# The start of a hybrid decoder step: the first product's weights in two halves, its first 24 matmuls ahead of x's third piece, and half of x's sums rebuilt on GpSimd

## The chip, the cores and the metric

The kernel runs on one core of a Trainium2 chip. The metric is the device time of one execution in microseconds (us), median of several. Engines are named as the profile names them: PE is TensorE (PEld its weight loads), DVE is VectorE, ACT is ScalarE, POOL is GpSimd, SP the engine whose queue issues most transfers.

## What is computed

One layer of a decoder over 512 prompt tokens and 8 x 4 sample tokens (544 columns in all), model width 2048. The input x is multiplied by `w_in` (2048 x 18952), whose columns are the queries, keys, values and gates of two parallel branches: an mLSTM with 4 heads and a windowed attention with 32 query and 4 key/value heads. The branches are gated, projected (`w_proj_m`, `w_proj_a`), merged, multiplied by `w_out`, added to x and normalised. The part that matters here is the first step of it:

```python
u = jnp.einsum('btd,dc->btc', x, w_in)      # all projections of x
q_m, k_m, v_m, o_m, z_m, q_a, k_a, v_a, z_a, g_m, g_a, i_pre, f_pre = split(u)
```

## The kernel before

**Arithmetic.** Every fp32 operand is held as a high part (a cast to the reduced format fp32r on ACT, `hi`) and a low part (the operand minus the high part, on DVE, `lo`). A product of weights w and activations x is three matmuls per 128-deep slice k: wh·xh, wh·xl, wl·xh. `split` makes wh and wl of half a weight tile (8 slices, 128 x 1024): one ACT cast (L200) and one DVE subtraction (L201). `hilo` does the same for activations (L245, L246). `products` issues the three matmuls for 8 slices and for the two halves of the 544 columns (272 each), all on L210: 48 matmuls for half a weight tile.

**Start.** x comes in five transfers over its 2048 columns: 256, 256, 512, 512, 512 wide (L307), on SP's queue, in slices k of 128 columns: pieces one and two hold k = 0, 1 and 2, 3, piece three k = 4 to 7. Behind piece two stands the first half of the first product's weights (`raw0[0]`, 512 KB), behind piece four the second half. The sample rows come on ACT's queue (L300). After 20 warm-up transposes (L295) the loop over `g` from 0 to 7 takes two slices each: four PE transposes per slice into a PSUM bank (L328; four such banks, pool `sm`), then `hilo` from PSUM into the activation tiles `a11` and `a21` (k < 8: first and second half of the columns) or `xk2` (k of 8 and more). The sample rows' transposes (L331) stand at k = 2 and fill a bank of their own, which is read out a quarter at a time, at every odd `g`.

**Sums of x.** Later products run in a scheme with seven half products (`paired`, L718) whose activations are sums and differences of x's quarters. Three fp32 tiles gather them: `n2r` = first half of the columns for k < 8 (rebuilt from high and low part on POOL, L351), `s1r` = second half for k < 8 (copied by ACT from PSUM: L337, L348), `n3r` = n2r + s1r (POOL, L359). When k of 8 and more arrive, DVE replaces s1r by x minus s1r (L342, L355). Afterwards `x_sums` (L573) takes s1r from n2r on POOL (L576) and makes high and low parts s1, n3 and n2, the low parts on DVE (L246, L586).

**First products.** `gemm` (L224) is called twice (L613) for the attention values (`VA_`, 128 columns each): first product, into two `bank` tiles, with the weights raw0[0] and raw0[1]; second product with raw0[2] and a later load, with the gate pre-activations (`gates_half`, L395, matmuls on L409) between. The split of the first weights is placed behind the cast of k = 3 (`state["k3"]`). Then come the paired products, L685 (wh) and L687 (wl), which fill most of the kernel; weight sums for them are made by DVE (L665) or by an adding transfer that POOL issues (L663).

**Gates.** `gates` (L412) is a generator that makes small rows of 4 partitions step by step beside the paired products; four DVE copies (L508 to L511) gather rows into `T1`, which PE transposes later (L530).

**Order.** Each engine runs its own queue in order. A planner lays the queues out when the program is built, by program order, priorities and modelled times; `tc.high_priority` lifts a block, and `tc.issue_after(ins)` puts a block's instructions behind `ins` where they are on the same engine. Waits between engines follow from the data.

Of the kernel before, what the change touches and what calls it, by code (L numbers as in the profile page):

```python
# [21 lines left out]
SEQ = 512  # L22
# [52 lines left out]
def _build(tc, nc, i, o, es):  # L75
# [35 lines left out]
    def r32(ap):  # L111
        return ap.bitcast(F32)
# [81 lines left out]
    def split(raw, p=None, tags=("wh", "wl"), parts=1):  # L194
# [3 lines left out]
        n = 8 // parts  # L198
        for k in range(0, 8, n):
            state["cast"] = A.copy(wh[:, k:k + n], raw[:, k:k + n])  # L200
            state["split"] = V.tensor_tensor(out=wl[:, k:k + n], in0=raw[:, k:k + n], in1=r32(wh[:, k:k + n]),  # L201
                                             op=ALU.subtract)
        return wh, wl

    def products(ps, half, wh, wl, xh, xl, cols, every=8):
        for kk in range(8):
            k = half * 8 + kk
            for n, (a, b) in enumerate(((wh, xh), (wh, xl), (wl, xh))):
                for f, c, w in cols:
                    PE.matmul(ps[f][:, :w], a[:, kk], b(k, c, w),  # L210
                              start=(k == 0 and n == 0), stop=(k == 15 and n == 2))
            if (k + 1) % every == 0:
                tick()

# [5 lines left out]
    def mm():  # L220

        return [bank(), bank()]

    def gemm(wv, c0, xh, xl, cols=EVEN, raws=(None, None), every=8, prio=0, before=None, parts=(1, 1),  # L224
             ps=None, behind=None):
        ps = ps or mm()
        for half in range(2):
            if before:
                before(half)
            raw = raws[half] or load_half(wv, c0, half)  # L230
            if prio:
                with tc.high_priority(offset=prio):
                    wh, wl = split(raw, parts=parts[half])
            else:
                with tc.issue_after(behind.ins) if behind and half == 0 else ExitStack():
                    wh, wl = split(raw, parts=parts[half])
            products(ps, half, wh, wl, xh, xl, cols, every)
        return ps

# [4 lines left out]
    def hilo(src, hi, lo, eng=None):  # L244
        state["x_cast"] = A.copy(hi, src)  # L245
        (eng or V).tensor_tensor(out=lo, in0=src, in1=r32(hi), op=ALU.subtract)  # L246
# [41 lines left out]
    def two_k(ch):  # L288
        return slice(ch * 2, ch * 2 + 2)
# [23 lines left out]
    state["load"] = xdma  # L313
# [6 lines left out]
    for t_ in gate_w:  # L320
        G.memset(r32(t_[:]), 0.0)
    pxs = bank()
    for g in range(8):
        for q in range(2):
            k = g * 2 + q
            pt = sm()
            for t in range(4):
                PE.transpose(pt[:, t * 128:t * 128 + 128], xt[k][:, t], ident)  # L328
            if k == 2:
                for c in range(4):  # L330
                    PE.transpose(pxs[:, c * 128:c * 128 + 128], xs[:, c], ident)  # L331
            if k < 8:
                hilo(pt[:, 0:HT], a11[0][:, k], a11[1][:, k])
                hilo(pt[:, HT:SEQ], a21[0][:, k, 0:SEQ - HT], a21[1][:, k, 0:SEQ - HT])
                if k == 3:
                    state["k3"] = state["x_cast"]
                A.copy(s1r[:, k, 0:SEQ - HT], pt[:, HT:SEQ])  # L337
            else:
                hilo(pt[:], xk2[0][k // 4 - 2][:, k % 4, 0:SEQ], xk2[1][k // 4 - 2][:, k % 4, 0:SEQ])
                x_cast = state["x_cast"]  # L340
                c = (slice(None), k - 8, slice(0, SEQ - HT))
                state["x_end"] = V.tensor_tensor(out=s1r[c], in0=pt[:, HT:SEQ], in1=s1r[c], op=ALU.subtract)  # L342
        if g % 2:
            k4 = slice((g // 2) * 4, (g // 2) * 4 + 4)
            src = pxs[:].rearrange("p (c q t) -> p q c t", c=4, q=4)[:, g // 2]
            if g < 4:
                hilo(src, *(a21[p][:, k4, SEQ - HT:HT] for p in range(2)))
                A.copy(s1r[:, k4, SEQ - HT:HT], src)  # L348
                for ch in (g - 1, g):
                    ks_ = two_k(ch)  # L350
                    G.tensor_tensor(out=n2r[:, ks_], in0=r32(a11[0][:, ks_]), in1=r32(a11[1][:, ks_]), op=ALU.add)  # L351
            else:
                hilo(src, *(xk2[p][g // 2 - 2][:, :, SEQ:T] for p in range(2)))
                c = (slice(None), slice(k4.start - 8, k4.stop - 8), slice(SEQ - HT, HT))
                V.tensor_tensor(out=s1r[c], in0=src, in1=s1r[c], op=ALU.subtract)  # L355
        if g == 3:
            for ch in range(4):
                ks_ = two_k(ch)
                G.tensor_tensor(out=n3r[:, ks_], in0=n2r[:, ks_], in1=s1r[:, ks_], op=ALU.add)  # L359
    esXr.close()  # L360
    t544 = pool(esG, "t544", 13)

# [49 lines left out]
    def gates(ps):  # L412
# [95 lines left out]
        V.tensor_copy(T1[0:4, :], ap)  # L508
        V.tensor_copy(T1[32:36, 0:384], A1)
        V.tensor_copy(T1[64:68, 0:256], A2)  # L510
        V.tensor_copy(T1[96:100, 0:128], A3)  # L511
        yield
        A.copy(nM[0:4], M)
        for q in (32, 64):
# [96 lines left out]
            gates_half(gates_ps, half)  # L611

    for kk in range(2):  # L613
        ps = gemm(win, VA_ + kk * 128, xh, xl, raws=((raw0[0], raw0[1]), (raw0[2], None))[kk], every=4, prio=500 * kk,
                  before=gates_between if kk else None, ps=[sm(), sm()] if kk else None, behind=state["k3"])
# [1318 lines left out]
```

## Time and profile before

| what | us |
|---|---|
| median of 3 runs | 2463.73 (2461.29 to 2463.8) |
| the profiled execution | 2463.52 |
| its span in the profile | 2461.7 |

A row of a timeline gives start and duration in us, engine, line of the kernel, operation, output<-input by the program's names, shape and count; where the engine was idle before, the idle time and what ended it stand in brackets. A row of the waits gives who waited for whom, with total, number and longest. A row of a stretch gives its length and, for each engine, busy time and number of instructions, then the granted PE clock (1.00 is full speed), the share of DMA and GB/s. PE instructions overlap in their durations, so the spacing of their starts is their price; the chain of waits shows it as time per group.

### The profile page before, as it was taken

What the parts mean: (1) busy time and instruction counts of PE and PEld (TensorE: products, weight loads), DVE (VectorE), ACT (ScalarE), POOL (GpSimd) and SP (SyncE); (2) the same over time, 40 slices, a digit from 0 to 9 for tenths busy, and PEclk for the clock granted to TensorE, in tenths of its full rate; (3) what the DMA queues carried; (4) which work ended last, traced back from release to release, by engine and by line L of the source; (5) the groups of instructions that cost most, each with busy time, mean ns of one, the idle gap of its engine ahead of it and who ended that gap; (6) DMA issues with size and microseconds to landing.
All of it is one profiled execution on the core that took longest, in us unless ns stands there. A gap on an engine that the chain in (4) does not pass through costs nothing.

```text
span 2461.7 us, 48799 instructions
## 1 busy us (share of the span) xinstructions
PE 2434.9 (99%) x19446; PEld 2381.0 (97%) x19446; DVE 1877.5 (76%) x2813; ACT 1214.4 (49%) x1992; POOL 511.0 (21%) x478
## 2 busy tenths in 40 slices
PE   8999999999999999999999999999999999999997
PEld 8999999999999999999999999999999999999997
DVE  7768888888888887887877888777865654777657
ACT  5456676676676565433433434444633333334431
POOL 3114334333333330221111221211000000110111
PEclk9999999999999999999999999999999999999998
DMA  6876676766666654577687586677755546888876
GB/s 177 198 175 158 159 166 143 164 158 154 160 150 165 152 150 115 152 226 240 180 253 241 164 244 214 182 229 219 248 171 173 185 149 210 223 221 252 220 222 189
DMA packets 555660, 464.72 MB, mean 189 GB/s; under 512 B 43688, under 2 KB 452440, under 8 KB 555176
## 3 DMA queue, kind: packets, MB, share of 16 engines
q1 hardware_dynamic: 538536, 402.09, 55.4%
q0 software_dynamic: 15696, 57.15, 12.1%
q8 instruction: 153, 2.51, 0.4%
q10 hardware_dynamic: 1200, 2.36, 0.3%
q14 instruction: 75, 0.61, 0.1%
HBM read 319.06 MB, written 96.31 MB: 169 GB/s over the span
## 4 chain that ended last, share of the span: by engine, by line
PE 95%; DMA 3%; DVE 1%; issue 1%; ACT 0%; SPq 0%; DVEq 0%; POOL 0%; POOLq 0%
PE bank L685 47%; PE bank L687 23%; PE bank L210 11%; PE sm L1438 2%; PE sm L210 1%; PE bank L1250 1%; PE sm L1470 1%; PE sm L795 1%; PE sm L1483 1%; PE sm L841 1%; DMA tx<-d_y 1%; DMA ty<-d_y 1%; PE sm L1800 1%; PE sm L1255 1%; PE sm L821 1%
## 5 line engine op out<-in xcount | busy, mean ns | idle before, releaser
L200 ACT CAST wh<-raw 128x1024 fp32r<-128x1024 f32 x632 | 662.7, 1049 | 844.5 <-PE bank L685 698.8
L201 DVE TENSOR_TENSOR wl<-raw,wh 128x1024 fp32r<-128x1024 f32 x632 | 790.9, 1252 | 201.9 <-ACT wh L200 184.9
L685 PE MATMUL bank<-xk,wh 128*128 128x272 f32 x2336 | 322.0, 289 | 0.0
L665 DVE TENSOR_TENSOR raw<-raw,raw 128x1024 f32<-128x1024 f32 x238 | 300.9, 1265 | 5.2 <-DMA raw<-in_w_in 1.5
L685 PEld LDWEIGHTS bank<-xk,wh 128*128 128x128 f32 x2336 | 302.8, 188 | 2.0 <-issue 1.5
L704 POOL TENSOR_TENSOR ev<-p,ev 128x272 f32<-128x272 f32 x82 | 118.5, 1446 | 440.2 <-ACT ev L703 397.9
L685 PE MATMUL bank<-n2h,wh 128*128 128x272 f32 x656 | 170.6, 292 | 0.0
L687 PE MATMUL bank<-xk,wl 128*128 128x272 f32 x1168 | 170.1, 288 | 0.0
L685 PE MATMUL bank<-s1h,wh 128*128 128x272 f32 x656 | 169.7, 291 | 0.0
L685 PE MATMUL bank<-n3h,wh 128*128 128x272 f32 x656 | 169.3, 290 | 0.2 <-ACT wh L200 0.2
L685 PE MATMUL bank<-n2l,wh 128*128 128x272 f32 x656 | 168.6, 289 | 0.0
L685 PE MATMUL bank<-n3l,wh 128*128 128x272 f32 x656 | 167.7, 288 | 0.0
L685 PE MATMUL bank<-s4h,wh 128*128 128x272 f32 x656 | 167.6, 289 | 0.0
L685 PE MATMUL bank<-s1l,wh 128*128 128x272 f32 x656 | 167.3, 287 | 0.0
L685 PE MATMUL bank<-s4l,wh 128*128 128x272 f32 x656 | 167.0, 287 | 0.0
L687 PEld LDWEIGHTS bank<-xk,wl 128*128 128x128 f32 x1168 | 155.7, 188 | 0.1
L685 PE MATMUL bank<-a11h,wh 128*128 128x272 f32 x584 | 150.3, 289 | 0.0
L685 PE MATMUL bank<-a11l,wh 128*128 128x272 f32 x584 | 149.5, 288 | 0.0
L210 PE MATMUL bank<-bl,wh 128*128 128x272 f32 x704 | 147.7, 288 | 0.0
L210 PE MATMUL bank<-bh,wl 128*128 128x272 f32 x704 | 147.5, 290 | 0.0
L210 PE MATMUL bank<-bh,wh 128*128 128x272 f32 x704 | 147.3, 288 | 0.0
L663 POOL DMA_DIRECT2D raw<-raw x90 | 78.1, 868 | 291.4 <-DVE ev L712 200.9
(492 smaller groups left out, 5667.0 us busy)
## 6 DMA issues: line engine op xcount, KB each, us to landing
raw<-in_w_in SPq DMA_DIRECT2D x296, 512.0 KB
raw<-raw POOLq DMA_DIRECT2D x90, 512.0 KB, 5.0
C<-in_state_mlstm_C SPq DMA_DIRECT2D x32, 1024.0 KB
out<-C SPq DMA_DIRECT2D x64, 512.0 KB
raw<-in_w_proj_a SPq DMA_DIRECT2D x32, 512.0 KB
raw<-in_w_proj_m SPq DMA_DIRECT2D x32, 512.0 KB
raw<-in_w_out SPq DMA_DIRECT2D x32, 512.0 KB
d_v<-ev SPq DMA_DIRECT2D x16, 272.0 KB
```

Of the source, the lines that this page charges most:

```text
L200: state["cast"] = A.copy(wh[:, k:k + n], raw[:, k:k + n])
L201: state["split"] = V.tensor_tensor(out=wl[:, k:k + n], in0=raw[:, k:k + n], in1=r32(wh[:, k:k + n]), op=ALU.subtract)
L210: PE.matmul(ps[f][:, :w], a[:, kk], b(k, c, w), start=(k == 0 and n == 0), stop=(k == 15 and n == 2))
L663: G.dma_start(out=w[out][:], in_=w[b][:], accum_op=ALU.add)
L665: V.tensor_tensor(out=w[out][:], in0=w[a][:], in1=w[b][:], op=ALU.add)
L685: PE.matmul(ps, wh[:, k], x(p, k), start=(first and k == 0 and p == 0), stop=False, skip_group_check=True)
L687: state["end"] = PE.matmul(ps, wl[:, k], x(0, k), start=False, stop=(k == 7), skip_group_check=True)
L704: G.tensor_tensor(out=c22, in0=p1, in1=c11, op=ALU.subtract)
L795: PE.matmul(pp[:, c0 + w0:c0 + 256], qs[a][:, j * 128:j * 128 + 128], kx[:, k0:k0 + 256 - w0], start=(n == 0), stop=(n == 1))
L821: PE.transpose(pt[:, b * 128:b * 128 + 128], s_[:, b, 128:256], ident)
L841: PE.matmul(po[:, b * 128:b * 128 + n], VA[:, b], p_[:, 2 * b:2 * b + n // 128], start=(b == 0 and m == 0), stop=(b == 3 and m == 1), skip ...
L1438: PE.matmul(pp[:, 0:258], a[:, b * 128:b * 128 + 128], b_[:, b, f], start=(b == 0 and n == 0), stop=(b == 3 and n == 2))
```

## The change

Five edits go together.

- The first weights' half is loaded in two quarters (`load_part` with slices 0 to 3, then 4 to 7): the first behind x's first piece, the second behind x's second piece. `split_part` casts and subtracts one quarter.
- The loop over `g` becomes a function `x_group`, called with the first product's matmuls between: group 0, split of the first quarter, 12 matmuls (k = 0, 1), group 1, 12 matmuls (k = 2, 3), split of the second quarter, groups 2 and 3, 24 matmuls (k = 4 to 7), groups 4 to 7. Group 1's transposes are placed behind the samples' transposes, its casts of the first column half behind the first quarter's cast, and group 2's first transposes behind the 24 matmuls.
- The samples' transposes move from k = 2 to k = 0, and the first read-out of their bank from g = 1 to g = 0.
- ACT no longer copies s1r from PSUM; POOL rebuilds it from a21's high and low part, chunk by chunk between n2r and n3r (four more POOL instructions of 128 x 544).
- The four copies into `T1` move from DVE to POOL.

```diff
         xdma = nc.sync.dma_start(t_, xp_src[:, :, c0:c0 + n])
         xt += [t_[:, :, c:c + 128] for c in range(0, n, 128)]
-        if c0 == 256:
-            raw0.append(load_half(win, VA_, 0))
+        if c0 == 0:
+            raw0.append(wr.tile([128, 8, 128], F32, tag="raw", name=nm("raw")))
+            load_part(raw0[0], win, VA_, 0, slice(0, 4))
+        elif c0 == 256:
+            load_part(raw0[0], win, VA_, 0, slice(4, 8))
         elif c0 == 1024:
             raw0.append(load_half(win, VA_, 1))
...
-    for g in range(8):
+    def x_group(g, behind=None, cast=None):
         for q in range(2):
             k = g * 2 + q
             pt = sm()
             for t in range(4):
-                PE.transpose(pt[:, t * 128:t * 128 + 128], xt[k][:, t], ident)
-            if k == 2:
+                with tc.issue_after(behind.ins) if behind and q == 0 else ExitStack():
+                    PE.transpose(pt[:, t * 128:t * 128 + 128], xt[k][:, t], ident)
+            if k == 0:
                 for c in range(4):
-                    PE.transpose(pxs[:, c * 128:c * 128 + 128], xs[:, c], ident)
+                    state["samples_in"] = PE.transpose(pxs[:, c * 128:c * 128 + 128], xs[:, c], ident)
             if k < 8:
-                hilo(pt[:, 0:HT], a11[0][:, k], a11[1][:, k])
+                with tc.issue_after(cast.ins) if cast else ExitStack():
+                    hilo(pt[:, 0:HT], a11[0][:, k], a11[1][:, k])
                 hilo(pt[:, HT:SEQ], a21[0][:, k, 0:SEQ - HT], a21[1][:, k, 0:SEQ - HT])
-                if k == 3:
-                    state["k3"] = state["x_cast"]
-                A.copy(s1r[:, k, 0:SEQ - HT], pt[:, HT:SEQ])
...
-        if g % 2:
+        if g in (0, 3, 5, 7):
...
-                A.copy(s1r[:, k4, SEQ - HT:HT], src)
-                for ch in (g - 1, g):
-                    ks_ = two_k(ch)
-                    G.tensor_tensor(out=n2r[:, ks_], in0=r32(a11[0][:, ks_]), in1=r32(a11[1][:, ks_]), op=ALU.add)
...
-        if g == 3:
-            for ch in range(4):
+        if g in (1, 3):
+            for ch in (g - 1, g):
                 ks_ = two_k(ch)
+                for r_, (h_, l_) in ((n2r, a11), (s1r, a21)):
+                    G.tensor_tensor(out=r_[:, ks_], in0=r32(h_[:, ks_]), in1=r32(l_[:, ks_]), op=ALU.add)
                 G.tensor_tensor(out=n3r[:, ks_], in0=n2r[:, ks_], in1=s1r[:, ks_], op=ALU.add)
+    ps0 = mm()
+
+    def first_products(k0, k1):
+        products(ps0, 0, *w0, xh, xl, EVEN, ks=slice(k0, k1))
+
+    w0 = [wp.tile([128, 8, 128], F32R, tag=t_, name=nm("wh")) for t_ in ("wh", "wl")]
+    x_group(0)
+    with tc.issue_after(state["x_cast"].ins):
+        split_part(raw0[0], *w0, slice(0, 4))
+    first_products(0, 2)
+    x_group(1, behind=state["samples_in"], cast=state["cast"])
+    first_products(2, 4)
+    with tc.issue_after(state["x_cast"].ins):
+        split_part(raw0[0], *w0, slice(4, 8))
+    for g in range(2, 4):
+        x_group(g, behind=state["product"] if g == 2 else None)
+    first_products(4, 8)
+    for g in range(4, 8):
+        x_group(g)
...
-        V.tensor_copy(T1[0:4, :], ap)
-        V.tensor_copy(T1[32:36, 0:384], A1)
-        V.tensor_copy(T1[64:68, 0:256], A2)
-        V.tensor_copy(T1[96:100, 0:128], A3)
+        G.tensor_copy(T1[0:4, :], ap)
+        G.tensor_copy(T1[32:36, 0:384], A1)
+        G.tensor_copy(T1[64:68, 0:256], A2)
+        G.tensor_copy(T1[96:100, 0:128], A3)
```

`gemm` loses its `parts` and `behind` arguments and gets the halves to run: the first product's call runs its second half only, into `ps0`.

More of the change, by code (lines that the diff above doesn't have):

```diff
@@ L192, in load_half, with split_part, split @@
         return raw
-    def split(raw, p=None, tags=("wh", "wl"), parts=1):
+    def split_part(raw, wh, wl, ks):
+        state["cast"] = A.copy(wh[:, ks], raw[:, ks])
+        state["split"] = V.tensor_tensor(out=wl[:, ks], in0=raw[:, ks], in1=r32(wh[:, ks]), op=ALU.subtract)
+    def split(raw, p=None, tags=("wh", "wl")):
         p = p or wp
@@ L197, in split, with products @@
         wl = p.tile([128, 8, 128], F32R, tag=tags[1], name=nm("wl"))
[L198 to L202, printed above, removed]
+        split_part(raw, wh, wl, slice(0, 8))
         return wh, wl
-    def products(ps, half, wh, wl, xh, xl, cols, every=8):
-        for kk in range(8):
+    def products(ps, half, wh, wl, xh, xl, cols, every=8, ks=slice(0, 8)):
+        for kk in range(ks.start, ks.stop):
             k = half * 8 + kk
@@ L222, in mm, with gemm @@
         return [bank(), bank()]
-    def gemm(wv, c0, xh, xl, cols=EVEN, raws=(None, None), every=8, prio=0, before=None, parts=(1, 1),
-             ps=None, behind=None):
+    def gemm(wv, c0, xh, xl, cols=EVEN, raws=(None, None), every=8, prio=0, before=None, ps=None, halves_=(0, 1)):
         ps = ps or mm()
-        for half in range(2):
+        for half in halves_:
             if before:
@@ L230, in gemm @@
             raw = raws[half] or load_half(wv, c0, half)
[L231 to L236, printed above, removed]
+            with tc.high_priority(offset=prio) if prio else ExitStack():
+                wh, wl = split(raw)
             products(ps, half, wh, wl, xh, xl, cols, every)
```

11 lines of the change are left out of this document (6 added, 5 removed).

## The prediction

> **What bounds the kernel now.** I read the page first: busy time of each engine over the span.
>
> ```profile
> span 2461.7 us, 48799 instructions
> PE 2434.9 (99%) x19446; PEld 2381.0 (97%) x19446; DVE 1877.5 (76%) x2813; ACT 1214.4 (49%) x1992; POOL 511.0 (21%) x478
> ```
>
> TensorE is the bound, and only 26.8 us of the span are its own idle time. A change at the start is therefore worth the TensorE time that it saves there, provided nothing later eats it. The view of waits, for TensorE alone, says where the idle time has a cause (total, times, longest):
>
> ```profile
> PE sm L295 <- DMA cc<-in_consts: 3.3, 1, 3.3
> PE sm L328 <- DMA xr<-in_x_prompt: 3.1, 1, 3.1
> ...
> PE bank L210 <- DVE xk L246: 0.5, 1, 0.5
> ```
>
> The first is the launch, which nothing here touches. The second is the place of the change: the transposes of x's third piece wait for their transfer, and the first product's matmuls stand behind them. Stretches of that stage, with busy time per engine, granted clock, DMA share and GB/s:
>
> ```profile
> 10.45:13.45 3.00, 0.00 (x0) 0.01 (x1) 2.38 (x7) 2.98 (x11) 2.19 (x3) 1.00 1.04 386
> 13.45:14.35 0.90, 0.88 (x8) 0.90 (x9) 0.71 (x2) 0.57 (x3) 0.90 (x1) 1.00 1.05 373
> 14.35:18.15 3.80, 3.80 (x22) 3.80 (x21) 2.49 (x7) 2.83 (x11) 3.76 (x4) 0.56 1.12 343
> ...
> 24.60:30.30 5.70, 5.22 (x44) 5.00 (x42) 5.70 (x11) 5.00 (x11) 2.73 (x2) 1.00 0.51 83
> 30.30:53.70 23.40, 23.38 (x188) 23.37 (x188) 23.40 (x39) 12.33 (x27) 3.39 (x3) 1.00 0.43 111
> ```
>
> Three things stand here. TensorE does nothing for 3.0 us. Right after, its clock is granted at 0.56 for 3.8 us, so 3.8 x 0.44 = 1.7 us more are lost although it counts as busy. And from 24.6 to 53.7 us VectorE is busy without a gap (5.70 of 5.70, 23.40 of 23.40). With the 0.5 us wait for VectorE, the prize is at most 3.0 + 1.7 + 0.5 = 5.2 us, 0.21% of the time.
>
> **The change part by part.** Unit prices first, from the chain of waits (start, us, what):
>
> ```profile
> 23.23 0.45 PE sm L328 x4
> ...
> 46.71 4.03 PE bank L409 x32
> ...
> 53.91 2.00 PE bank L685 x16
> ...
> 56.90 2.00 PE bank L685 x16
> ```
>
> So a transpose costs 0.11 us and a 272-column matmul 0.126 us at full clock; 24 matmuls are 3.0 us.
>
> *Weights in two halves ahead of x's second piece.* TensorE's weight loads show when the first two pieces are there:
>
> ```profile
> 7.42 1.19 PEld L328 LDWEIGHTS sm<-cc,xr 128*128 128x128 f32 x8
> 8.89 0.86 PEld L328 LDWEIGHTS sm<-cc,xr 128*128 128x128 f32 x8 [0.28 <-DMA xr<-in_x_prompt]
> ```
>
> The second piece lands at 8.89 us. A quarter of a megabyte more ahead of it, at the 343 to 386 GB/s of the stretches above, is 0.7 us: 9.6. The extra issue on SP's queue (one of its kind:
>
> ```profile
> 2.20 0.51 SPq L187 DMA_DIRECT2D raw<-in_w_in  x1
> ```
>
> 0.51 us) I put at nothing: the DMA engines are saturated (share above 1), so issues run ahead of them; without that cover it would be half a microsecond on the third piece as well. The bytes ahead of the third piece are unchanged, so it still lands near 13.4. Until 9.6 TensorE does the first piece and the four sample transposes that have moved forward (7.42 + 1.19 + 4 x 0.11 = 9.05), waits 0.55, and does the second piece by 10.5, against 10.42 before: nothing lost.
>
> *The split of the first half, and 24 matmuls ahead of the third piece.* ScalarE, VectorE and GpSimd rows (start, us, instruction):
>
> ```profile
> 8.45 0.82 ACT L245 CAST a11h<-sm 128x272 fp32r<-128x272 f32 x2 [3.22 <-PE sm L328]
> ...
> 11.66 1.05 ACT L200 CAST wh<-raw 128x1024 fp32r<-128x1024 f32 x1
> ```
>
> ```profile
> 12.73 1.23 DVE L201 TENSOR_TENSOR wl<-raw,wh 128x1024 fp32r<-128x1024 f32 x1 [0.61 <-ACT wh L200]
> ...
> 22.77 0.69 DVE L246 TENSOR_TENSOR xk<-sm,xk 128x512 fp32r<-128x512 f32 x1 [1.86 <-ACT xk L245]
> ...
> 25.25 0.68 DVE L246 TENSOR_TENSOR xk<-sm,xk 128x512 fp32r<-128x512 f32 x1
> ...
> 26.16 0.68 DVE L246 TENSOR_TENSOR xk<-sm,xk 128x512 fp32r<-128x512 f32 x1
> ...
> 27.47 2.20 DVE L201 TENSOR_TENSOR wl<-raw,wh 128x1024 fp32r<-128x1024 f32 x1
> ...
> 32.93 0.39 DVE L342 TENSOR_TENSOR r<-sm,r 128x240 f32<-128x240 f32 x1
> ...
> 33.34 2.51 DVE L246 TENSOR_TENSOR s1l<-r,s1h 128x544 fp32r<-128x544 f32 x2
> ```
>
> ```profile
> 9.82 2.64 POOL L351 TENSOR_TENSOR n2r<-a11h,a11l 128x544 f32<-128x544 f32 x2 [6.68 <-DVE a11l L246]
> 13.27 3.20 POOL L359 TENSOR_TENSOR r<-n2r,r 128x544 f32<-128x544 f32 x2 [0.81 <-ACT r L348]
> ...
> 19.65 3.40 POOL L359 TENSOR_TENSOR r<-n2r,r 128x544 f32<-128x544 f32 x2 [0.47 <-ACT r L337]
> 25.41 1.37 POOL L576 TENSOR_TENSOR n2r<-n2r,r 128x544 f32<-128x544 f32 x1 [2.35 <-DVE r L342]
> 27.23 1.35 POOL L576 TENSOR_TENSOR n2r<-n2r,r 128x544 f32<-128x544 f32 x1 [0.45 <-DVE r L342]
> ...
> 33.46 1.81 POOL L576 TENSOR_TENSOR n2r<-n2r,r 128x544 f32<-128x544 f32 x1 [0.44 <-DVE wg L404]
> ```
>
> ScalarE casts the first group from 8.45 and, behind its last piece, half of wh (half of 1.05: 0.55 us), done at about 10.45: in time for the first product at 10.5. The subtraction for wl, 0.65 us by half of 1.23, is another matter. The rows at 27.23 and 27.47 show it: a VectorE instruction with both inputs in SBUF takes 2.20 us instead of 1.23 when a GpSimd add has begun just before it; begun first (12.73), it takes its 1.23 and the add behind it is longer (13.27: 1.60 each against 1.32). I read that as the two shutting each other out, at about 1.0 us a collision. The Trainium skill, "GPSIMD Engine Reference", section "Key points", says the same in kind: GpSimd shares its SBUF interfaces with VectorE, and contends with VectorE instructions that have two SBUF inputs. It gives no price; by it every such pair collides, which is the third rival below. The row at 27.47 bears it out once.
>
> GpSimd's first add again starts near 9.9 us and holds until 11.3. So I take one collision for this first subtraction: wl at 11.95 (bounds: 11.1 with no collision, 13.3 if a second add also gets in ahead). TensorE starts at 10.5, stops after four products, resumes at 11.95 and needs 20 x 0.126 = 2.5 us: 14.45. The third piece, landed at 13.4, is then taken up 1.0 us later than before, but with 24 products done: 3.0 - 1.0 = **2.0 us** gained. No gap exceeds 1 us, so I take the clock as full through 14 to 18 us: **1.7 us** (bounds: nothing, if the clock falls all the same, and 1.7).
>
> *Half of x's sums on GpSimd.* Ten ScalarE copies go (L337, L348); ScalarE isn't the bound here, so they are worth only time for the casts, counted above. Four adds of 1.35 us join eight: 8 x 1.35 + 4 x 1.65 = 17.4 us from 9.9, plus some 2.3 us in which VectorE's splits of weights get in: the last n3r at about 29.6, against 19.65 + 3.40 = 23.05 before. Queued behind this on VectorE are the subtractions into s1r (L342) of the last two chunks of k, and behind them the last low parts of x that TensorE needs. Before, VectorE's stage of k = 8 to 15 ran from 22.77 to 33.3. Now I start it at 20.4 (low parts of k = 4 to 7 until 18.3, the weights' second half until 20.4) and give it 8 x 0.91 (the spacing of 25.25 and 26.16) + 0.4 for samples + 2.2 for a collided split + 0.6 waiting for GpSimd = 10.5: 30.9, so 2.4 us earlier. TensorE comes 3.7 us earlier, so it may wait a little for k = 14 and 15; the next product's matmuls fill most of that. I take 0.3 us off (bounds: 0 and 2).
>
> *What is late next.* At the paired products the split for the second step stands thus:
>
> ```profile
> 53.19 1.05 ACT L200 CAST wh<-raw 128x1024 fp32r<-128x1024 f32 x1 [2.65 <-PE sm L210]
> ```
>
> It ends at 54.24 and TensorE uses it at 56.90 (chain above): 2.66 us of slack. VectorE 2.4 us earlier plus this slack covers a TensorE up to 5.0 us earlier. Beyond, TensorE runs dense, and what it waits for (stores and reloads of its own results) moves with it.
>
> *Four copies into T1 from VectorE to GpSimd.* First and last of four on VectorE, then GpSimd around them:
>
> ```profile
> 84.92 0.42 DVE L508 COPY t<-t 4x544 f32<-4x544 f32 x1
> ...
> 87.10 0.22 DVE L511 COPY t<-t 4x128 f32<-4x128 f32 x1
> ```
>
> ```profile
> 85.93 0.86 POOL L663 DMA_DIRECT2D raw<-raw  x1
> 96.39 0.84 POOL L663 DMA_DIRECT2D raw<-raw  x1 [9.59 <-DMA raw<-in_w_in]
> ```
>
> GpSimd has no such copy in the trace; for 1312 columns together I bound it by nothing and by its 1.35 us per 544 columns, 3.3 us, and take 2. They lie in a gap of 9.59 us; TensorE has no wait there before and none after: nothing. If they are put ahead of the adding transfer at 85.93, that transfer is up to 3.3 us late, and a step's weights with it, of which a slack like the 2.66 us above leaves under 1 us on TensorE.
>
> **Sum:** 2.0 + 1.7 - 0.3 = 3.4 us. The profiled execution took 2463.52 us (span 2461.7, 1.8 around it), so 2460.1. The median of the runs shown is 2463.73, so the two agree within 0.2 us.
>
> **Rivals.**
> 1. *Full recovery.* GpSimd's first add doesn't meet the first subtraction, the 24 products run dense from 10.5 to 13.5, and the 0.5 us at 30 goes too: 3.0 + 1.7 + 0.5 - 0.1 = 5.1 us, **2458.4**. For it: ScalarE has the cast ready in time. Against: VectorE has no idle time to spare from 24.6 on.
> 2. *The products stand ahead but find no weights.* The subtraction is shut out twice (13.3), so TensorE reaches the third piece at 15.8, 2.35 us late: 3.0 - 2.35 + 1.7 - 0.3 = 2.0 us, **2461.5**. The change then does not do what it says. For it: four more adds keep GpSimd busy without a break from 9.9 to 29.6. Against: at 33.34, VectorE's second subtraction followed directly at the add's end (33.46 + 1.81 = 35.27; 33.34 + 2.51 = 35.85).
> 3. *Slower: GpSimd shuts out VectorE through its full stretch.* Besides four splits of weights, eight subtractions for s1l and n3l have both inputs in SBUF. If all twelve collide at 1.0 us, that is eight more than the four in my sum: VectorE is 8 - 2.4 = 5.6 us later than before, less the slack of 2.66: TensorE loses 2.9 us, **2466.4**. It decides from the point where collisions beyond my four exceed 2.4 + 2.66, about the tenth in all. For it: GpSimd's adds now reach to 29.6 and four more follow, to about 35. Against: VectorE's instructions that read PSUM kept their length beside GpSimd (the L246 rows at 25.25 and 26.16), and they are most of the stage.
>
> **How the numbers follow.** Forecast (2.3 to 4.6 us gained) 0.48, full recovery 0.22, rival 2 0.17, rival 3 0.13. A difference of 0.2%, 4.9 us, is about what a measurement of this kernel can tell from no change. Faster by more than that (under 2458.8): most of rival 1 and the edge of the forecast, 0.22. Slower by more (over 2468.7): the far part of rival 3, where the order of later instructions shifts against TensorE too, 0.09. Within: 0.69. The range takes in the bounds 11.1 and 13.3 of the first subtraction, the clock's loss coming back in part, and rivals 1 and 2, and leaves out rival 3 and the end of rival 1: 2457.6 to 2464.2.
>
> **What would show each step.** Right: no TensorE wait for x's third piece over 1 us; the granted clock near 1 from 14 to 18 us; 24 products (L210's line) ahead of the third piece's transposes; the first paired matmul near 50.3 us instead of 53.9. Wrong: a TensorE wait for wl before 14 us much longer than 1.5; a clock of 0.5 to 0.6 after 14 us; wl subtractions near 2.2 us three or more times; VectorE waiting for GpSimd before L342; a second wait for VectorE near 25 to 30 us longer than 1 us; the first paired matmul early, but a wait for ScalarE or VectorE after it that gives the time back.

## The result, and the profile after

The changed kernel takes 2474.49 us (median of 6 runs, 2470.35 to 2475.98), the kernel before 2462.80 on the same chip: a ratio of 1.0046, 95% interval 1.0036 to 1.0057, so 11.7 us slower by the medians. The forecast was 2460.1 and its range ended at 2464.2. The profiled execution of the changed kernel took 2474.02 us. Lines shift by the diff: L685 is now L700, L663 is L678, L665 is L680, L704 is L719, L576 is L591, L404 is L419, L409 is L424, L201 is L196, L246 is L241, L342 is L339, L359 is L354, the copies into T1 (L508 to L511) are L523 to L526, and the scan L462 is L477. In the kernels of the experiments that are built on the changed one, lines are up to five higher still.

The page, its first lines:

```profile
span 2472.2 us, 48781 instructions
...
PE 2437.3 (99%) x19446; PEld 2382.0 (96%) x19446; DVE 1881.5 (76%) x2810; ACT 1211.4 (49%) x1983; POOL 525.1 (21%) x486
```

The span is 10.5 us longer, and TensorE's busy time only 2.4: most of the loss is idle time, 34.9 us against 26.8. The same stretches as before the change, and two later ones (busy time per engine, granted clock, DMA share, GB/s), first of the changed kernel, then the last one of the kernel before:

```profile
10.45:13.45 3.00, 2.30 (x17) 1.84 (x16) 2.88 (x8) 1.98 (x7) 1.57 (x2) 1.00 1.04 386
14.35:18.15 3.80, 3.80 (x34) 3.80 (x33) 2.64 (x7) 2.28 (x9) 3.80 (x4) 1.00 1.12 346
...
75.00:100.00 25.00, 19.39 (x151) 18.66 (x149) 20.48 (x37) 9.85 (x15) 8.14 (x9) 0.96 0.63 132
100.00:130.00 30.00, 27.91 (x214) 27.91 (x214) 19.12 (x23) 11.50 (x13) 3.92 (x4) 0.92 0.76 188
```

```profile
100.00:130.00 30.00, 30.00 (x242) 29.82 (x241) 17.51 (x27) 12.77 (x19) 4.90 (x5) 1.00 0.76 188
```

The change does what it says where it was made: TensorE works in 10.45 to 13.45, and the clock of 0.56 behind it is 1.00. The loss lies at 75 to 130 us, where the edit has only four small copies. TensorE's view of waits (total, times, longest) names the new ones (a line `...` stands for rows left out):

```profile
PE bank L700 <- ACT wh L195: 7.8, 3, 6.7
PE sm L1270 <- DMA VB<-d_kv: 3.6, 1, 3.6
...
PE bank L424 <- DVE wg L419: 1.5, 1, 1.5
PE bank L210 <- DVE a21l L241: 1.2, 1, 1.2
```

The second is a reload at 1.6 ms, which all kernels here have in some length; it makes ends of spans differ by 2 us or so from one execution to the next, and I leave it out. To place the rest I counted TensorE's matmuls in order of start and took the start of the n-th in each trace less that in the trace of before (us; all have 19446):

| n (time in before) | before the change | after |
|---|---|---|
| 88 (20.8) | 0 | -3.0 |
| 208 (36.1) | 0 | -0.1 |
| 564 (80.4) | 0 | +1.0 |
| 708 (98.7) | 0 | +9.5 |
| 5000 (632) | 0 | +9.4 |

So 3.0 us are gained by 18 us, given back by 36, and 9.5 lost between 78 and 108. The give-back, on VectorE and then on GpSimd (start, us, instruction):

```profile
11.13 1.35 DVE L196 TENSOR_TENSOR wh<-raw,wh 128x512 fp32r<-128x512 f32 x1
...
19.16 2.21 DVE L196 TENSOR_TENSOR wl<-raw,wh 128x1024 fp32r<-128x1024 f32 x1 [0.66 <-ACT wh L195]
...
30.13 2.71 DVE L419 TENSOR_TENSOR wg<-xs,wg 128x32 fp32r<-128x32 f32 x2
32.77 1.34 DVE L339 TENSOR_TENSOR r<-sm,r 128x240 f32<-128x240 f32 x4
```

```profile
28.80 1.37 POOL L354 TENSOR_TENSOR r<-n2r,r 128x544 f32<-128x544 f32 x1
30.13 1.38 POOL L591 TENSOR_TENSOR n2r<-n2r,r 128x544 f32<-128x544 f32 x1
31.44 1.35 POOL L354 TENSOR_TENSOR r<-n2r,r 128x544 f32<-128x544 f32 x1
```

GpSimd has no gap between its adds here, and two subtractions of 128x32, tiny work, take 2.71 us beside them, 1.42 and 1.37, each as long as the add that it stands beside: VectorE is through when 31.44 + 1.35 = 32.79 is reached (30.13 + 2.71 = 32.84). The gates' products (L424) wait 1.5 us for that. Earlier, at 21.75, TensorE's wait of 1.2 us is for a low part of a21 (L241) that stands on VectorE behind the split that took 2.21 us at 19.16. These two waits are 2.7 of the 2.9 us given back.

The great loss, followed back from its end: TensorE, the chain of waits before it, GpSimd, and SyncE's queue of the changed kernel.

```profile
102.09 3.58 PE L700 MATMUL bank<-xk,wh 128*128 128x272 f32 x16 [6.71 <-ACT wh L195]
```

```profile
93.39 7.53 DMA raw<-raw
100.99 1.05 ACT wh L195
```

```profile
88.15 3.62 POOL L719 TENSOR_TENSOR ev<-p,ev 128x272 f32<-128x272 f32 x1 [7.73 <-DVE t L505]
91.72 0.63 POOL L523 COPY t<-t 4x544 f32<-4x544 f32 x1
...
93.39 0.59 POOL L678 DMA_DIRECT2D raw<-raw  x1
```

```profile
89.33 0.41 SPq L187 DMA_DIRECT2D raw<-in_w_in  x1
91.16 0.41 SPq L671 DMA_DIRECT2D raw<-in_w_in  x1
```

The adding transfer is issued at 93.39 (85.93 before), behind three of T1's copies and a subtraction of the paired scheme on GpSimd, c22 = p1 - c11 (L719), of 3.62 us, and it takes 7.53 us to land. ScalarE's cast waits for it, TensorE for the cast, 6.71 us; the next 16 matmuls take 3.58 us instead of 16 x 0.126 = 2.0, at a granted clock of 0.59. That makes the 8.3 us between the 660th matmul (+1.2) and the 708th (+9.5).

Of the 7.5 us by which the issue is late, the copies themselves are 1.7 (91.72 to 93.39). The subtraction starts 2.95 us later than in the kernel before, where it took 0.78 from 85.20, and lasts 2.84 longer. VectorE's row of the changed kernel beside it, then GpSimd's row of x1 (below), which has the copies on VectorE again:

```profile
88.09 1.21 DVE L196 TENSOR_TENSOR wl<-raw,wh 128x1024 fp32r<-128x1024 f32 x1
```

```profile
87.03 0.82 POOL L719 TENSOR_TENSOR ev<-p,ev 128x272 f32<-128x272 f32 x1 [7.92 <-DVE t L505]
```

Without the copies VectorE comes to its split at 88.09, just ahead of GpSimd's subtraction at 88.15, which is stretched; in x1 the split starts at 88.50, behind the copies and behind the end of that subtraction.

### The profile page after: what moved, and what is told of

It is laid out like the page before. It is cut to its first block, busy times and chain, and to the rows that moved or that the text cites. A ratio compares the mean times of both kernels' runs of the same rounds, so it can differ in the third digit from the quotient of the medians.

```text
span 2472.2 us, 48781 instructions
## 1 busy us (share of the span) xinstructions
PE 2437.3 (99%) x19446; PEld 2382.0 (96%) x19446; DVE 1881.5 (76%) x2810; ACT 1211.4 (49%) x1983; POOL 525.1 (21%) x486
## 3 DMA queue, kind: packets, MB, share of 16 engines
q0 software_dynamic: 15696, 57.15, 12.1%
## 4 chain that ended last, share of the span: by engine, by line
PE 94%; DMA 2%; DVE 2%; issue 0%; POOL 0%; ACT 0%; SPq 0%; DVEq 0%; POOLq 0%; ACTq 0%
PE bank L700 46%; PE bank L702 22%; PE bank L210 13%; PE sm L1453 2%; PE sm L210 1%; PE bank L1265 1%; PE sm L1485 1%; PE sm L810 1%; PE sm L1498 1%; PE sm L856 1%; PE sm L1815 1%; PE sm L836 1%; PE sm L1270 1%; DMA raw<-raw 1%; DMA raw<-in_w_in 0%
## 5 line engine op out<-in xcount | busy, mean ns | idle before, releaser
L195 ACT CAST wh<-raw 128x1024 fp32r<-128x1024 f32 (+1 forms) x633 | 662.5, 1047 | 850.7 <-PE bank L700 693.8
L196 DVE TENSOR_TENSOR wl<-raw,wh 128x1024 fp32r<-128x1024 f32 x631 | 790.1, 1253 | 211.0 <-ACT wh L195 192.7
L700 PE MATMUL bank<-xk,wh 128*128 128x272 f32 x2336 | 323.8, 290 | 6.7 <-ACT wh L195 6.7
L700 PEld LDWEIGHTS bank<-xk,wh 128*128 128x128 f32 x2336 | 304.2, 189 | 9.0 <-ACT wh L195 6.9
L680 DVE TENSOR_TENSOR raw<-raw,raw 128x1024 f32<-128x1024 f32 x238 | 301.8, 1270 | 5.5 <-DMA raw<-in_w_in 1.2
L719 POOL TENSOR_TENSOR ev<-p,ev 128x272 f32<-128x272 f32 x82 | 122.4, 1493 | 433.8 <-ACT ev L718 388.2
L700 PE MATMUL bank<-n2h,wh 128*128 128x272 f32 x656 | 171.0, 292 | 0.0
L700 PE MATMUL bank<-s1h,wh 128*128 128x272 f32 x656 | 169.7, 291 | 0.9 <-ACT wh L195 0.9
L700 PE MATMUL bank<-n3h,wh 128*128 128x272 f32 x656 | 169.1, 290 | 0.2 <-ACT wh L195 0.2
L700 PE MATMUL bank<-n2l,wh 128*128 128x272 f32 x656 | 169.1, 289 | 0.0
L700 PE MATMUL bank<-s4h,wh 128*128 128x272 f32 x656 | 167.9, 289 | 0.1
L700 PE MATMUL bank<-n3l,wh 128*128 128x272 f32 x656 | 167.6, 288 | 0.0
L700 PE MATMUL bank<-s1l,wh 128*128 128x272 f32 x656 | 167.2, 287 | 0.0
L700 PE MATMUL bank<-s4l,wh 128*128 128x272 f32 x656 | 167.1, 287 | 0.0
L700 PE MATMUL bank<-a11h,wh 128*128 128x272 f32 x584 | 150.3, 289 | 0.0
L700 PE MATMUL bank<-a11l,wh 128*128 128x272 f32 x584 | 149.5, 288 | 0.0
L678 POOL DMA_DIRECT2D raw<-raw x90 | 78.2, 869 | 294.6 <-DVE ev L727 190.9
```

Of the source, the lines that this page charges most:

```text
L195: state["cast"] = A.copy(wh[:, ks], raw[:, ks])
L196: state["split"] = V.tensor_tensor(out=wl[:, ks], in0=raw[:, ks], in1=r32(wh[:, ks]), op=ALU.subtract)
L678: G.dma_start(out=w[out][:], in_=w[b][:], accum_op=ALU.add)
L680: V.tensor_tensor(out=w[out][:], in0=w[a][:], in1=w[b][:], op=ALU.add)
L700: PE.matmul(ps, wh[:, k], x(p, k), start=(first and k == 0 and p == 0), stop=False, skip_group_check=True)
L719: G.tensor_tensor(out=c22, in0=p1, in1=c11, op=ALU.subtract)
```

## The experiments

The kernels of a group ran on the same chip beside the kernel before, whose median was 2463.15 us (x1 to x4), 2461.63 (x5 to x8) and 2463.00 (x9 to x11); I compare by the ratio, with "+6.6" for a median 6.6 us over that of before. The whole change has its own, 2462.80. Half a width of the intervals is 2 to 3 us. The last three columns are starts of TensorE's n-th matmul less those of before, in the profiled executions: one of each kernel, which need not lie at its median (x1's took 2471.55, x6's 2477.35; x8's 2465.40 and x11's 2464.47 are their quickest).

| kernel | ratio (95%) | us | 208th | 564th | 708th |
|---|---|---|---|---|---|
| the whole change | 1.0046 (1.0036 to 1.0057) | +11.7 | -0.1 | +1.0 | +9.5 |
| x1 order + sums | 1.0027 (1.0017 to 1.0037) | +6.6 | -1.6 | -0.3 | +4.2 |
| x2 T1 | 1.0010 (1.0001 to 1.0019) | +2.7 | -0.2 | -0.2 | +2.9 |
| x3 sums | 0.9999 (0.9991 to 1.0008) | -0.4 | -1.1 | -1.2 | -0.7 |
| x4 order | 0.9995 (0.9987 to 1.0004) | -1.6 | -2.2 | -2.2 | -2.3 |
| x5 order + T1 | 1.0012 (1.0003 to 1.0021) | +2.9 | -3.4 | -3.4 | +1.5 |
| x6 whole, T1 behind the transfer | 1.0049 (1.0036 to 1.0061) | +12.1 | -0.5 | +0.4 | +10.3 |
| x7 order + half the sums | 1.0004 (0.9996 to 1.0013) | +1.7 | -2.3 | -2.3 | -2.4 |
| x8 x1, c22 on VectorE | 1.0023 (1.0015 to 1.0032) | +5.6 | -1.4 | -0.3 | +2.8 |
| x9 order + T1 behind the transfer | 0.9987 (0.9978 to 0.9996) | -2.7 | -2.3 | -2.3 | -2.5 |
| x10 x7 + T1 behind the transfer | 0.9995 (0.9986 to 1.0004) | -1.5 | -1.4 | -1.4 | -1.7 |
| x11 x6, second c22 on VectorE | 1.0027 (1.0018 to 1.0036) | +6.8 | -1.3 | -0.5 | +2.2 |

**One part at a time.** I began with three theories: P, T1's copies stand ahead of the adding transfer; L, the additional adds on GpSimd shut VectorE out; M, the new order itself does harm.

x1, the whole change with T1's copies back on VectorE:

```diff
-        G.tensor_copy(T1[0:4, :], ap)
...
+        V.tensor_copy(T1[0:4, :], ap)
...
```

> The changed kernel with the four T1 copies on VectorE again (new order and sums on GpSimd kept). Theory P, the copies stand in GpSimd's queue ahead of an adding transfer and make it late: the 6.7 us wait of TensorE near 95 us goes, and with it the slow clock after it, some 2.4 us; 8 to 10 us faster than the changed kernel, so within 2 us of the kernel before. Theory L, the extra adds on GpSimd shut VectorE out and make all of it late, and the copies only happen to stand there: 2 to 3 us faster than the changed kernel, still 7 or more slower than before.

x2, the kernel before with only T1's copies on GpSimd:

```diff
-        V.tensor_copy(T1[0:4, :], ap)
...
+        G.tensor_copy(T1[0:4, :], ap)
...
```

> The kernel before with only the four T1 copies moved to GpSimd. Theory P alone: 6 to 9 us slower than before, with a TensorE wait for a cast behind the adding transfer. Theory L: the transfer is late by the copies' 2.3 us, which the slack of that step covers: within 1 us of before.

x3, the kernel before with only s1r rebuilt on GpSimd:

```diff
-                A.copy(s1r[:, k, 0:SEQ - HT], pt[:, HT:SEQ])
...
+                    G.tensor_tensor(out=s1r[:, ks_], in0=r32(a21[0][:, ks_]), in1=r32(a21[1][:, ks_]), op=ALU.add)
```

> The kernel before with only s1r rebuilt on GpSimd in place of ScalarE's ten copies. Theory P: within 1 us of before. Theory L: GpSimd's adds reach to 30 us or later, VectorE's subtractions with two SBUF inputs collide more than twice, VectorE is 2 to 4 us later at 55 us: 2 to 5 us slower than before.

x4, the new order alone; on the changed kernel, T1's copies back on VectorE as in x1, and s1r copied by ScalarE:

```diff
+                A.copy(s1r[:, k, 0:SEQ - HT], pt[:, HT:SEQ])
...
+                A.copy(s1r[:, k4, SEQ - HT:HT], src)
...
-                for r_, (h_, l_) in ((n2r, a11), (s1r, a21)):
-                    G.tensor_tensor(out=r_[:, ks_], in0=r32(h_[:, ks_]), in1=r32(l_[:, ks_]), op=ALU.add)
+                G.tensor_tensor(out=n2r[:, ks_], in0=r32(a11[0][:, ks_]), in1=r32(a11[1][:, ks_]), op=ALU.add)
```

> Only the new order of the start (weights in two quarters, 24 matmuls ahead of the third piece); s1r copied by ScalarE and the T1 copies on VectorE as before. Both theories: the forecast's first two terms are left without the cost of GpSimd, 3 to 4 us faster than before. A third theory M, the order itself does harm (wl too late, x's third piece held back): no faster than before.

M falls by the trace: the order alone keeps 2.3 us of the 3.5 that it has at the 88th matmul, through the paired products (-2.3 at the 5000th). Its time, -1.6, is less than the 3 to 4 that were expected, and its interval takes in no change. T1 alone costs 2.7, between P's 6 to 9 and L's 1. The sums alone cost nothing that can be told, where L had 2 to 5; the two subtractions of 128x32 took 0.17 each there. But order and sums together (x1) cost 6.6, again between P's 2 and L's 7, and T1 on top of them 5 more: the parts do not add up, and neither theory fits all four.

**How T1 costs.** T1 alone is the clean case. SyncE's queue, GpSimd's and VectorE's rows of the kernel before, then of x2:

```profile
88.95 2.07 SPq L187 DMA_DIRECT2D raw<-in_w_in  x2
```

```profile
87.71 1.22 DVE L201 TENSOR_TENSOR wl<-raw,wh 128x1024 fp32r<-128x1024 f32 x1
```

```profile
86.90 0.41 SPq L187 DMA_DIRECT2D raw<-in_w_in  x1
```

```profile
85.66 1.21 DVE L201 TENSOR_TENSOR wl<-raw,wh 128x1024 fp32r<-128x1024 f32 x1
```

```profile
88.40 0.59 POOL L663 DMA_DIRECT2D raw<-raw  x1
```

```profile
DMA to landing us min/median/max: 7.3/7.3/7.3
```

Two things happen at once. The copies delay the adding transfer from 85.93 to 88.40. And VectorE, without them, does its next subtraction 2.05 us earlier, which frees a weight buffer, so SyncE's next load goes out at 86.90 instead of 88.95. The load is now ahead of the transfer, and the transfer lands 7.3 us after its issue (the last row; 4.7 in the kernel before). P, as I had stated it, has only the first of the two; x6 and x9 below tell what the second does.

x5, the new order with T1's copies on GpSimd, sums as before (x2's edit on x4):

> The new order and T1's copies on GpSimd, with half of x's sums copied by ScalarE as before the change. Theory A (costs add up: T1's place costs the same under either order): the order alone gave 2461.52, T1 alone 2.7 over the kernel before, so 2464.2 (2463.5 to 2465). Theory B (T1 costs more once TensorE runs ahead, since the slack of the adding transfer was used up): the 4.7 us that T1 cost on top of order and sums, 2466.2 (2465.5 to 2467).

+2.9 us over the kernel before, where A's 2464.2 was 1.1 over it and B's 2466.2 was 3.1 over: inside B's range and outside A's, though the interval, 2.2 us each way, takes in both. The traces say 1.5 - (-2.3) = 3.8 us for T1 under the new order, 2.9 under the old one: more, and less than the 5 on top of the sums. Its transfer, too, took 7.3 us.

x6, the whole change, with the copies queued behind the transfer:

```diff
-                G.dma_start(out=w[out][:], in_=w[b][:], accum_op=ALU.add)
+                state["acc"] = G.dma_start(out=w[out][:], in_=w[b][:], accum_op=ALU.add)
...
+        with tc.issue_after(state["acc"].ins):
+            G.tensor_copy(T1[0:4, :], ap)
...
```

> The whole change, with T1's four copies still on GpSimd but queued behind the adding transfer that they stand ahead of in the changed kernel. Theory P (their place in the queue is what costs): the 4.7 us between the changed kernel (2474.49) and the one with T1 on VectorE (2469.76) come back, 2469.8 (2468.5 to 2471), and TensorE's wait of 6.7 us near 102 is under 3. Theory C (the copies cost by taking GpSimd and its share of the port, wherever they stand): no more than a quarter comes back, 2473.3 or above.

Nothing comes back, as C had it. P as I had put it falls: the copies are out of the way, the transfer is issued 2.3 us earlier, and TensorE waits as long as before. GpSimd, SyncE, the transfer's landing, and the DMA queues between 91.2 and 95.5 us (packets, MB, share of 16 engines) in x6:

```profile
91.10 0.86 POOL L679 DMA_DIRECT2D raw<-raw  x1
```

```profile
88.71 0.41 SPq L187 DMA_DIRECT2D raw<-in_w_in  x1
```

```profile
DMA to landing us min/median/max: 9.2/9.2/9.2
```

```profile
q1 hardware_dynamic: 1032, 0.52, 44.4%
```

In the 4.3 us after the transfer's issue its queue, which is q0, moves nothing: only the loads' queue has a row. The transfer was still issued behind SyncE's load, because the subtraction ahead of it took 3.58 us, stretched as in the changed kernel. So a third theory, R: what decides is which is issued first, the adding transfer or SyncE's load; T1's copies matter because they can turn that order round. R and theory C (the copies cost by running on GpSimd at all) are told apart where the transfer gets ahead.

x9, the new order with T1's copies on GpSimd behind the transfer (x6's edit on x4):

> The new order, x's sums copied by ScalarE as before the change, T1's four copies on GpSimd but queued behind the adding transfer. Theory R (what costs is the adding transfer issued after SyncE's next weight load: the load's packets then go first and the transfer lands 7.3 us after its issue, not 4.8): the transfer is issued near 82.7, ahead of the load near 83.9, lands 4.8 us later, TensorE's 3.3 us wait goes, and the kernel is 1 to 3 us under the kernel before, as the order alone was (-1.6). Theory C (the copies cost by running on GpSimd, wherever they stand): 2 to 4 us over the kernel before, as with the copies ahead (+2.9).

```profile
83.16 0.85 POOL L680 DMA_DIRECT2D raw<-raw  x1
```

```profile
85.42 3.03 SPq L187 DMA_DIRECT2D raw<-in_w_in  x2
```

```profile
DMA to landing us min/median/max: 4.9/4.9/4.9
```

```profile
q0 software_dynamic: 144, 0.52, 57.9%
q1 hardware_dynamic: 209, 0.08, 27.5%
```

With the transfer first (83.16, load 85.42), its whole half megabyte moves between 83.2 and 88.5 us (the last two rows), it lands after 4.9 us, and the time is 2.7 us under the kernel before, where the copies ahead of it made it 2.9 over (x5). The two edits differ in the copies' place alone; with it the transfer goes out 2.3 us earlier than in x5 and the load 1.5 later. R holds and C falls. This is also the one kernel of the study whose interval lies under the kernel before: 2460.30 us, ratio 0.9987.

x11, x6 with the subtraction ahead of the transfer on VectorE:

```diff
-            G.tensor_tensor(out=c22, in0=p1, in1=c11, op=ALU.subtract)
+            state["c22"] = state.get("c22", 0) + 1
+            (V if state["c22"] == 2 else G).tensor_tensor(out=c22, in0=p1, in1=c11, op=ALU.subtract)
```

> The whole change with T1's copies behind the adding transfer, and the second paired work's p1 - c11, which took 3.58 us on GpSimd at 87.58 ahead of that transfer, on VectorE. Theory R: the transfer is issued by 88, ahead of SyncE's loads at 88.7 and 90.5, lands under 5.5 us later instead of 9.2, TensorE's wait of 6.7 us near 101 is under 4, and the time is 6 to 9 us over the kernel before (order and sums without T1 gave +6.6). Theory C or S (it is late for other reasons): 11 us or more over the kernel before.

```profile
86.13 0.85 POOL L679 DMA_DIRECT2D raw<-raw  x1 [7.20 <-DVE wl L196]
```

```profile
88.71 3.12 SPq L187 DMA_DIRECT2D raw<-in_w_in  x2
```

```profile
DMA to landing us min/median/max: 5.3/5.3/5.3
```

```profile
96.17 0.39 PE L701 MATMUL bank<-a11h,wh 128*128 128x272 f32 x1 [2.30 <-ACT wh L195]
```

The load stays at 88.71, the transfer comes to 86.13, and 6.7 us of wait become 2.30. The median is +6.8 against +12.1, what order and sums cost without T1. Its runs spread more (2464.47 to 2474.95, three of them under 2466, the others from 2468.85 on), and the profiled one is the quickest: I take the rows as what happens when the transfer gets ahead, not as what every run does. The profiled executions of all thirteen kernels agree with R: in the nine where the transfer was issued ahead of the load it landed after 4.6 to 5.3 us, in the four where it was behind (the whole change, x2, x5, x6) after 7.3 to 9.2.

**How order and sums cost.** x7 does half of the sums:

```diff
+                if k >= 4:
+                    A.copy(s1r[:, k, 0:SEQ - HT], pt[:, HT:SEQ])
...
-                for r_, (h_, l_) in ((n2r, a11), (s1r, a21)):
+                for r_, (h_, l_) in ((n2r, a11), (s1r, a21))[:2 if g == 1 else 1]:
```

> New order, T1 on VectorE, and only the first two of the four pieces of x's sums rebuilt on GpSimd, the other two copied by ScalarE as before the change. Theory L (GpSimd's unbroken run of adds at 27.4 to 32.6 shuts VectorE out): the run breaks up, the two 128x32 subtractions take 0.2 each again, VectorE is 3 us earlier at 55, and nearly all of the 8.2 us between order alone (2461.52) and order with all sums (2469.76) comes back: 2461.5 to 2463.5. Theory D (each add has its own price): half comes back, 2465.6 (2464.5 to 2467).

VectorE's rows of x1, then of x7:

```profile
28.71 2.67 DVE L419 TENSOR_TENSOR wg<-xs,wg 128x32 fp32r<-128x32 f32 x2
31.30 0.71 DVE L339 TENSOR_TENSOR r<-sm,r 128x240 f32<-128x240 f32 x2
32.68 0.72 DVE L339 TENSOR_TENSOR r<-sm,r 128x240 f32<-128x240 f32 x2 [0.67 <-POOL r L354]
```

```profile
30.81 0.18 DVE L423 TENSOR_TENSOR wg<-xs,wg 128x32 fp32r<-128x32 f32 x1
...
33.36 0.18 DVE L423 TENSOR_TENSOR wg<-xs,wg 128x32 fp32r<-128x32 f32 x1
```

In x1 VectorE is shut out for 2.67 us and then waits 0.67 for an n3r add that reads what it is to overwrite; both are gone in x7, as L said, and its trace follows the order alone (-2.3, -2.4). The time doesn't settle L against D by itself: +1.7, where L's 2461.5 to 2463.5 was 1.6 under to 0.4 over the kernel before, and D's 1.4 to 3.9 over. That is in D's range and outside L's, but the interval, 2.1 us each way, takes in both. x10 adds to it, half the sums on x9:

> The new order, half of x's sums rebuilt on GpSimd, T1's copies on GpSimd behind the adding transfer: the whole change with both suspected faults mended. Theory L with R: within 1.5 us of the kernel before or under it (half the sums with T1 on VectorE gave +1.7). Theory C: 3 us or more over the kernel before.

-1.5 against -2.7. So half of the sums costs 0.0009 of the time on x4 and 0.0008 on x9, some 2 us, and all of them cost 0.0032, 7.9 us. A price for each add would make that 4. Two pairs with intervals this wide make it likely and no more that the second half costs more than the first.

Where the lateness ends up: VectorE's last instruction before it turns to the gates, with the same copy next (L570, in x4 L571), in x1 and in x4.

```profile
55.22 0.72 DVE L241 TENSOR_TENSOR s4l<-n2r,s4h 128x544 fp32r<-128x544 f32 x1
```

```profile
51.29 1.22 DVE L681 TENSOR_TENSOR raw<-raw,raw 128x1024 f32<-128x1024 f32 x1
```

It ends at 55.94 in x1 and 52.51 in x4, 3.4 us apart, while TensorE is only 0.6 behind at the 208th matmul. VectorE carries the difference on. x8 asked whether the stretched subtraction c22 = p1 - c11 near 60, ahead of another adding transfer, makes it a loss (on x1):

```diff
-            G.tensor_tensor(out=c22, in0=p1, in1=c11, op=ALU.subtract)
+            (G if "c22" in state else V).tensor_tensor(out=c22, in0=p1, in1=c11, op=ALU.subtract)
+            state["c22"] = True
```

> Order and sums as in the changed kernel, T1 on VectorE, and the first paired work's subtraction p1 - c11 (2.96 us on GpSimd at 59.48, 1.45 in the kernel before) on VectorE. Theory Q (that subtraction, stretched beside VectorE's two, puts off the adding transfer behind it in GpSimd's queue, 62.39 against 59.65, and all that follows): the transfer is issued near 60 and half or more of the 8.2 us over order alone comes back, under 2466. Theory S (VectorE's own lateness of 4 us at 54, gained at 28 to 39, is what carries on): 2468.5 to 2470, the transfer's issue being beside the point.

```profile
61.47 0.86 POOL L678 DMA_DIRECT2D raw<-raw  x1 [2.62 <-DVE wl L196]
```

```profile
74.32 1.28 DVE L477 TENSOR_TENSOR_SCAN t<-t,t 4x544 f32<-4x544 f32 x1 [1.17 <-DMA t<-t]
```

+5.6 against x1's +6.6: inside S's 2468.5 to 2470 when set against the kernel before, which was at 2463.15 then and at 2461.63 now (+5.4 to +6.9). Q falls: taken off GpSimd, the subtraction stands behind VectorE's own, the transfer is 0.9 us earlier only, and the scan still waits for its row of the gates. In all five kernels with the new order and all the sums (the whole change, x1, x6, x8, x11) that scan stands ahead of both adds (L680) into the next steps' weights, in the other eight between the two; and in those five alone TensorE waits near 78 us, 0.6 to 0.9 us, for the cast behind the first add. The second place is near 97 us. ScalarE and TensorE in x1:

```profile
93.83 0.66 ACT L519 ACTIVATE t<-t 4x544 f32<-4x544 f32 x1
...
95.54 1.03 ACT L195 CAST wh<-raw 128x1024 fp32r<-128x1024 f32 x1
```

```profile
96.62 0.39 PE L700 MATMUL bank<-a11h,wh 128*128 128x272 f32 x1 [2.22 <-ACT wh L195]
```

The adding transfer is in time here (issued at 87.80, ahead of the load at 89.76, landed 4.9 us later), and TensorE waits 2.22 us all the same, for a cast that stands on ScalarE behind four activations of the gates; in x4 the first of them starts at 87.56, and TensorE doesn't wait. x8 and x11 wait 2.3 us for the same cast. Why the planner turns the scan and the adds round, and how much of the 6.6 us each place is, wasn't tried and stays open.

## Why the prediction was wrong

**Weights in two halves, 24 matmuls ahead of the third piece: right in kind, a little large.** With the clock's 1.7 I had 3.7 us here, and 3.0 are there at the 88th matmul, so some 1.3 for the term of 2.0; in x4 it is 3.5. The collision that I put on the first subtraction is there too: 1.35 us at 11.13 for 0.65 worked out.

**The clock: right.** 1.00 in 14.35 to 18.15.

**Half of x's sums: the 0.3 us is the first term that failed.** From the 88th matmul to the 208th the changed kernel gives back 2.9 us, and the order without the sums (x4) 1.3. I had VectorE's stage end at 30.9, 2.4 us before the old one; in the changed kernel its last L339 ends at 32.77 + 1.34 = 34.11, 0.8 after it. I had counted four collisions, all of splits of weights, at about 1 us each, and one of them in this stage. In these rows the price is set by GpSimd's add, not by VectorE's instruction: in x1 two subtractions of 128x32 took 2.3 us more than the 2 x 0.18 that they take in x7, where the adds do not follow one another without a gap. And the end of TensorE's wait was not the end of the cost, since VectorE stayed late.

**The slack of 2.66 us and "beyond, TensorE runs dense": wrong.** The first paired matmul starts at 53.53 in the changed kernel, not at 50.3. The slack that I read at the second paired step did hold, but it wasn't the tightest one. Tighter were the places at 79 and 98 us, where a step's weights hang on an add in VectorE's queue, on an adding transfer, and on a cast behind the gates' activations on ScalarE; I had not looked at them because TensorE had no wait there before.

**Four copies into T1 at nothing, or under 1 us: the step that failed worst.** I had named the very place, "ahead of the adding transfer at 85.93", and priced it by the delay alone, less a slack read elsewhere. On its own the part costs 2.7 us, on top of the rest about 5. The delay (2.5 us in x2) was sized well; the transfer's own time was held constant, and it went from 4.7 to 7.3 us since a load overtook it. Taking the copies off VectorE is what let that load start 2.05 us earlier, and I had costed that side at nothing. In the changed kernel that side also put VectorE's split ahead of GpSimd's subtraction, 3.62 us in place of 0.82, so that the transfer was late by more than the copies.

**Rival 3** (GpSimd shuts out VectorE) named a cause that is real, at 2466.4 and a chance of 0.13. Its place was wrong: it would have made TensorE wait at the paired step, and instead the lateness was handed on to 79 and 98 us. Of the 11.7 us, x1's 6.6 are of its kind, and only with the new order: the sums alone cost nothing. No rival had the transfer. The one sentence that came near is the chance of 0.09 for over 2468.7, with "the order of later instructions shifts against TensorE too"; the range left it out.

## What to carry to other kernels

Before work is taken off an engine, look at what waits for its next instruction: here a subtraction came 2 us earlier, freed a buffer, and so started a load ahead of a transfer that was on the path to TensorE. In a queue that issues transfers, put nothing ahead of the issue that can stand behind it: with the new order, the same four copies make the kernel 2.9 us slower than before when they stand ahead of the issue, and 2.7 faster when behind it. And a slack holds for the place where it was read; a part that makes an engine late must be followed to each later place where that engine's queue meets the critical one.

## What the runs showed of the hardware

- An adding transfer of 512 KB, issued by GpSimd, took 4.6 to 5.3 us from issue to landing in the nine kernels where it was issued before the next load of SyncE, and 7.3 to 9.2 in the four where after it; in 4.3 us after its issue none of its packets moved (x6) while the loads' queue moved 0.52 MB. The Trainium skill, "DMA: Bandwidth & Descriptors", section "Queues, rings and completion order", states that a DMA engine takes turns between the queues it has work for, a packet at a time. By that the two would share as soon as both have work. The traces show little of it: in x2 11 packets of the transfer moved beside 883 of the loads in the 4.0 us after its issue. What holds the later one back is open; T1's copies, which follow the issue in x9 and x11 as in x6, don't.
- Beside GpSimd adds without a gap, two VectorE subtractions of 128x32 took 2.67 us together in x1 and 2.71 in the changed kernel, against 0.18 each in x7. The Trainium skill, "GPSIMD Engine Reference", section "Key points", names the contention for VectorE instructions with two SBUF inputs, which these are; the traces agree, and add that a short one can last as long as the whole add beside it (1.37 to 1.42 us each, with adds of 1.33 to 1.38).
- A TensorE idle of 6.7 us was followed by 16 matmuls in 3.58 us, and a mean granted clock of 0.92 in 100 to 130 us; in the kernel before it is 1.00 there. Not every wait was followed so: after 2.2 us in x1 (at 96.62) the next 4.8 us had a clock of 0.65, after 2.3 in x8 and 3.1 in x2 the next 4.0 us had 1.00. So part of what the profiled executions differ by at the 708th matmul is the clock; what decides it isn't shown.
